# A transformer layer on one core: the context's first combination is rounded earlier, and one norm moves behind the last of seven products

## The chip, the core and the metric

The kernel runs on one core of a Trainium2 chip. The metric is the device time in microseconds (us) of one execution; the number reported is the median of several runs.

The engines go by short names: PE (TensorE, matmuls; PEld is its weight load), DVE (VectorE), ACT (ScalarE), POOL (GpSimd) and SP, whose queue issues the DMAs. Each works through its own queue in order and waits for the others through semaphores.

## The reference, cut to what matters

```python
def swiglu(h, w1, w3, w2):
    return (jax.nn.silu(h @ w1) * (h @ w3)) @ w2

def reference(...):
    ...
    x = x + 0.5 * m_l[2][:, None, :] * swiglu(modulate(rms_norm(x, norm1_w[i]), m_l[0], m_l[1]), ffn1_w1[i], ffn1_w3[i], ffn1_w2[i])
    ctx = ctx + 0.5 * m_c[2][:, None, :] * swiglu(modulate(rms_norm(ctx, norm1_w[i]), m_c[0], m_c[1]), ffn1_w1[i], ffn1_w3[i], ffn1_w2[i])
    y_l, y_c = token_mixing(modulate(rms_norm(x, norm2_w[i]), m_l[3], m_l[4]),
                            modulate(rms_norm(ctx, norm2_w[i]), m_c[3], m_c[4]), w_in[i], ...)
    x = x + m_l[5][:, None, :] * y_l
    x = x + 0.5 * m_l[8][:, None, :] * swiglu(modulate(rms_norm(x, norm3_w[i]), ...), ffn2_w1[i], ffn2_w3[i], ffn2_w2[i])
    ...
return rms_norm(x, final_norm_w)
```

One layer: a feed-forward block on 1024 latent tokens and on 256 context tokens (width 1024, hidden width 2816), a token mixing step whose latent scans start from the context's scan states, and a second feed-forward block on the latent tokens. Everything is float32. This case is about the second half of the first feed-forward block (the product with `w2`), and the norm (`norm2_w`) between it and the token mixing.

## The kernel before, in words

**Numbers in two parts.** A float32 tile is rounded to a high part on ACT (`whi`, `hh`; line 435) and the rest is taken on DVE (`wlo`, `hl`; line 436). `mm3` then makes three matmuls of a product: high with high (L440), low with high (L441) and high with low (L442). Together, the two instructions are called a split here.

**Seven products.** The tokens come in halves of 512 (groups 0 and 1 latent, group 2 the context). A big product of latent tokens is cut into two by two blocks and made with seven block products instead of eight, from sums and differences of blocks. `hidden` goes over pairs of hidden blocks f = 2, 4, ..., 20 (NF = 22) and makes, per pair, one chain of seven products with `w1` and one with `w3`, then the silu product and the sums that the next stage needs, which it stores to DRAM (`gd`). The adaLN columns (`ada`, line 511) are computed on DVE beside it. Scratch tiles of this stage are the 19 buffers with the tag `s`; a pair takes 14.

**The context's combinations.** The context's hidden values lie in DRAM (`cgd`) too. `ctx_comb(b)` loads four blocks (four DMAs), makes four differences on DVE and stores them (four DMAs), for b = 0, 1, 2; it runs after the pairs f of the tuple `COMB`. `ctx_load(i, b)` loads one combination for product i, and `ctx_split(i, b)` splits it.

**The product with w2.** Its seven products come in the order 1, 6, 5, 7, 3 (in `back_ctx`), then 2, then 4, each a loop over 11 pairs p (NP) of hidden blocks. A pair needs a split of its token block (`hh`, `hl`, four slots in turn) and one of its weights (`whi`, `wlo`), and is used by 12 matmuls into four banks (`psa` or `psb`). In the first five products three more matmuls per pair, into a fifth bank, take the context along: weights `whi`, `wlo` against the context's split tile (`s`, later `ch`, `cl`). Latent results are added to `x` (line 883).

**What sets the order.** A hand-written table `plan` names work that is emitted after pair number i of these 77 pairs; 5*NP (`p2`) is the first pair of product 2, 6*NP (`p4`) that of product 4. Within what is emitted, a scheduler sets each engine's order by priorities; SP's order in `back_ctx` is the written one. `NLOW` puts parts 1 and 2 of the norm of group 1 at a lower priority. From the step after product 4 on (`ctx_k`, the context's keys, and what follows) the operations are recorded first and ordered by a planner; in the profile they all have line 147.

**A norm** (`norm_part`) has these parts. 0: squares, summed in `nacc` (ACT and DVE). 1: four matmuls with a one-column result (L573, eight passes in the trace) into a bank taken by `psN`, then the root in two steps, `nr` on DVE (L1628) and POOL (L1629). 2: four diagonal tiles `ndiag` on DVE (L583), four matmuls of 128 columns on them (L592), a copy `nrb` on ACT. 3 and on, one for each of 8 feature blocks: `nt` on DVE (L606), `hh` on ACT (L607), `hl` on DVE (L618). Group 2 goes through it in product 2. Group 1 has part 0 and parts 1 and 2 there as well, and its eight blocks among the first pairs of product 4. Group 0 follows in the recorded part.

## Time and profile before

| what | value |
|---|---|
| median of 3 runs | 2083.25 us (2082.26, 2083.25, 2085.28) |
| the profiled execution | 2083.51 us, its span 2081.7 us |
| mean granted TensorE clock | 0.994 |
| PE busy | 2057.9 us, 99% |
| DVE busy | 1519.5 us, 73% |
| ACT busy | 984.4 us, 47% |
| POOL busy | 69.0 us, 3% |
| DMA | 376.39 MB, mean 181 GB/s |

A timeline row has the start in us from the span's start, the length in us, the engine, the line, the operation, output <- inputs, shapes and a count; in brackets stands how long the engine sat idle before it and what ended that. Matmuls are pipelined: a row is 0.39 us long while the next starts 0.23 us later. A row of a stretch gives from:to and its length, then the busy us (and instructions) of PE, PEld, DVE, ACT and POOL, the granted clock, the busy share of the DMA engines and GB/s.

### The profile page before, as it was taken

What the parts mean: (1) busy time and instruction counts of PE and PEld (TensorE: products, weight loads), DVE (VectorE), ACT (ScalarE), POOL (GpSimd) and SP (SyncE); (2) the same over time, 40 slices, a digit from 0 to 9 for tenths busy, and PEclk for the clock granted to TensorE, in tenths of its full rate; (3) what the DMA queues carried; (4) which work ended last, traced back from release to release, by engine and by line L of the source; (5) the groups of instructions that cost most, each with busy time, mean ns of one, the idle gap of its engine ahead of it and who ended that gap; (6) DMA issues with size and microseconds to landing.
All of it is one profiled execution on the core that took longest, in us unless ns stands there. A gap on an engine that the chain in (4) does not pass through costs nothing.

```text
span 2081.7 us, 33747 instructions
## 1 busy us (share of the span) xinstructions
PE 2057.9 (99%) x12137; PEld 1747.0 (84%) x12137; DVE 1519.5 (73%) x2775; ACT 984.4 (47%) x1819; POOL 69.0 (3%) x107
## 2 busy tenths in 40 slices
PE   9999999999999998999999999999999999999998
PEld 8998888888878887898788988888888888888888
DVE  5888788898867777765576478767776666766576
ACT  5765434433445445566475246444434344345553
POOL 0000000000000000001021001000000000010000
PEclk9999999999999999999999999999999999999999
DMA  9765565567779765664233233242344444477764
GB/s 362 231 198 165 182 197 197 196 232 260 248 275 320 254 226 166 196 202 137 68 113 93 83 89 107 87 162 81 111 157 147 146 163 157 151 240 236 218 228 152
DMA packets 210089, 376.39 MB, mean 181 GB/s; under 512 B 23937, under 2 KB 44161, under 8 KB 209793
## 3 DMA queue, kind: packets, MB, share of 16 engines
q1 hardware_dynamic: 209632, 374.10, 55.1%
q8 instruction: 95, 1.56, 0.3%
q14 instruction: 74, 0.60, 0.1%
q10 hardware_dynamic: 288, 0.13, 0.0%
HBM read 292.74 MB, written 73.01 MB: 176 GB/s over the span
## 4 chain that ended last, share of the span: by engine, by line
PE 92%; DVE 3%; DMA 3%; issue 1%; ACT 1%; SPq 0%; POOL 0%; DVEq 0%; POOLq 0%; ACTq 0%
PE psa L147 24%; PE psb L147 11%; PE psa L440 10%; PE psa L442 10%; PE psa L441 10%; PE psb L442 9%; PE psb L440 9%; PE psb L441 9%; DMA raw<-in_w 1%; DMA hh<-in_w 1%; DMA raw<-gd 1%; DVE hl L436 1%; DVE x L883 0%; DVE wlo L436 0%; DVE nt L147 0%
## 5 line engine op out<-in xcount | busy, mean ns | idle before, releaser
L435 ACT ACTIVATE whi<-raw 128x512 fp32r<-128x512 f32 x385 | 242.9, 631 | 507.1 <-issue 177.7
L436 DVE TENSOR_TENSOR wlo<-raw,whi 128x512 fp32r<-128x512 f32 x385 | 265.0, 689 | 152.2 <-ACT whi L435 145.6
L440 PE MATMUL psa<-hh,whi 128*128 128x512 f32 x676 | 265.1, 392 | 1.3 <-ACT nrb L2100 0.7
L441 PE MATMUL psa<-hl,whi 128*128 128x512 f32 x676 | 264.3, 391 | 0.0
L442 PE MATMUL psa<-hh,wlo 128*128 128x512 f32 x676 | 264.3, 391 | 0.0
L147 PE MATMUL psa<-hh,whi 128*128 128x512 f32 (+1 forms) x664 | 234.4, 354 | 0.9 <-ACT whi L147 0.5
L147 PE MATMUL psa<-hh,wlo 128*128 128x512 f32 (+1 forms) x664 | 233.3, 352 | 0.1
L147 PE MATMUL psa<-hl,whi 128*128 128x512 f32 (+1 forms) x664 | 233.1, 352 | 0.0
L440 PE MATMUL psb<-hh,whi 128*128 128x512 f32 x584 | 227.6, 390 | 0.0
L442 PE MATMUL psb<-hh,wlo 128*128 128x512 f32 x584 | 227.2, 389 | 0.0
L441 PE MATMUL psb<-hl,whi 128*128 128x512 f32 x584 | 227.2, 389 | 0.0
L147 DVE TENSOR_TENSOR wlo<-raw,whi 128x512 fp32r<-128x512 f32 (+1 forms) x217 | 139.4, 663 | 103.9 <-ACT whi L147 92.7
L147 ACT ACTIVATE whi<-raw 128x512 fp32r<-128x512 f32 (+1 forms) x217 | 130.1, 610 | 148.4 <-PE psa L147 111.8
L440 PEld LDWEIGHTS psa<-hh,whi 128*128 128x128 f32 x676 | 127.7, 189 | 28.4 <-ACT s L734 1.0
L442 PEld LDWEIGHTS psa<-hh,wlo 128*128 128x128 f32 x676 | 127.7, 189 | 26.8
L441 PEld LDWEIGHTS psa<-hl,whi 128*128 128x128 f32 x676 | 127.9, 189 | 26.6
L147 PEld LDWEIGHTS psa<-hh,whi 128*128 128x128 f32 x664 | 126.1, 190 | 17.7 <-ACT whi L147 1.0
L147 PEld LDWEIGHTS psa<-hh,wlo 128*128 128x128 f32 x664 | 126.0, 190 | 15.2 <-DVE wlo L147 0.3
L147 PEld LDWEIGHTS psa<-hl,whi 128*128 128x128 f32 x664 | 125.9, 190 | 14.8 <-issue 0.2
L442 PEld LDWEIGHTS psb<-hh,wlo 128*128 128x128 f32 x584 | 109.6, 188 | 22.7
L440 PEld LDWEIGHTS psb<-hh,whi 128*128 128x128 f32 x584 | 109.6, 188 | 22.6
L441 PEld LDWEIGHTS psb<-hl,whi 128*128 128x128 f32 x584 | 109.6, 188 | 22.6
(490 smaller groups left out, 4217.0 us busy)
## 6 DMA issues: line engine op xcount, KB each, us to landing
raw<-in_w SPq DMA_DIRECT2D x316, 256.0 KB, 3.4
gd<-s SPq DMA_DIRECT2D x154, 256.0 KB, 2.9
raw<-gd SPq DMA_DIRECT2D x102, 256.0 KB, 3.1
ada<-in_adaT SPq DMA_DIRECT2D x48, 512.0 KB, 4.0
s<-in_w SPq DMA_DIRECT2D x66, 256.0 KB, 4.6
hh<-in_w SPq DMA_DIRECT2D x55, 256.0 KB, 4.7
sd<-s SPq DMA_DIRECT2D x44, 256.0 KB, 2.9
raw<-sd SPq DMA_DIRECT2D x44, 256.0 KB, 3.6
```

What stands on the lines that cost most here:

```text
L147: self.rec.add(self.eng, lambda: f(*map(get, a), **{x: get(v) for x, v in k.items()}), outs, ins, name, a, k)
L435: nc.scalar.activation(hi, src, AF.Copy)
L436: (eng or nc.vector).tensor_tensor(out=lo, in0=src, in1=hi.bitcast(F32), op=ALU.subtract)
L440: mm(ps, wa[0], xa[0], start=start, stop=False, skip_group_check=more)
L441: mm(ps, wa[0], xa[1], start=False, stop=False, skip_group_check=more)
L442: return mm(ps, wa[1], xa[0], start=False, stop=stop, skip_group_check=more)
```

## The change

The three `ctx_comb` steps go one pair earlier (after f = 10, 12, 14). The load of the context's first combination for product 1 moves from behind `hidden` to the end of pair f = 16, its split to the end of pair f = 18. The bank choice `psN = psB` and parts 1 and 2 of the norm of group 1 move from product 2 into product 4 (pairs 1 and 4), and its eight blocks from pairs 0 to 7 to pairs 6 to 9.

```diff
-    def hidden(self, f0, mods=lambda: None, hold=False, comb=()):
+    def hidden(self, f0, mods=lambda: None, hold=False, comb={}):
...
             if f in comb:
-                self.ctx_comb(comb.index(f))
+                comb[f]()
...
-        self.hidden(F0, lambda: mods(MPER), True, COMB)
-        mods(2 * len(todo))
         self.craw, self.cw, self.xw, self.nbank = {}, {}, {}, -1
-        self.ctx_load(1, 0)
-        self.ctx_split(1, 0, f1)
+        comb = {f: lambda b=b: self.ctx_comb(b) for b, f in enumerate(COMB)}
+        comb[NF - 6] = lambda: self.ctx_load(1, 0)
+        comb[NF - 4] = lambda: self.ctx_split(1, 0, f1)
+        self.hidden(F0, lambda: mods(MPER), True, comb)
+        mods(2 * len(todo))
...
-        plan[p2 + 8].append(lambda: norm2(1, 1))
-        plan[p2 + 9].append(lambda: norm2(1, 2))
-        plan[p2 + 10].append(lambda: setattr(self, "psN", self.psB))
+        plan[p4 + 1] += [lambda: setattr(self, "psN", self.psB), lambda: norm2(1, 1)]
+        plan[p4 + 4].append(lambda: norm2(1, 2))
         for k in range(KD):
             plan[p2 + 7 + k // 2].append(lambda k=k: norm2(2, 3 + k))
-            plan[p4 + k].append(lambda k=k: norm1(k))
+            plan[p4 + 6 + k // 2].append(lambda k=k: norm1(k))
...
-COMB = (12, 14, 16)
+COMB = (10, 12, 14)
```

What this does to the engines' order is seen at three places. First PE in product 1, in the third pair before and behind the first pair now; `psb_6069` is the context's bank, `s_6019`/`s_6020` (now `s_5689`/`s_5690`) the high and low part of its split tile. Before:

```order
L440 MATMUL psa_6067<-hh_1242_6141,whi_6149 128x512
L441 MATMUL psa_6067<-hl_1243_6142,whi_6149 128x512
L442 MATMUL psa_6067<-hh_1242_6141,wlo_6150 128x512
L440 MATMUL psb_6069<-whi_6086,s_6019 128x512
L441 MATMUL psb_6069<-wlo_6087,s_6019 128x512
L440 MATMUL psa_6068<-hh_1242_6141,whi_6149 128x512
L442 MATMUL psb_6069<-whi_6086,s_6020 128x512
L440 MATMUL psb_6069<-whi_6116,s_6019 128x512
```

Now, at the end of the first pair (`whi_6086`):

```order
L440 MATMUL psa_6068<-hh_1223_6070,whi_6086 128x512
L441 MATMUL psa_6068<-hl_1224_6071,whi_6086 128x512
L442 MATMUL psa_6068<-hh_1223_6070,wlo_6087 128x512
L440 MATMUL psb_6069<-whi_6086,s_5689 128x512
L441 MATMUL psb_6069<-wlo_6087,s_5689 128x512
L442 MATMUL psb_6069<-whi_6086,s_5690 128x512
L440 MATMUL psa_6065<-hh_1234_6108,whi_6116 128x512
```

The context's matmuls of the first pairs stood together in the third pair and stand now behind their own pairs. Second PE at the norm of group 1. Before, between product 2 (`psb_8126`) and product 4 (`psa_8566`):

```order
L442 MATMUL psb_8126<-hh_1872_8489,wlo_8498 128x512
L573 MATMUL psa_8426<-ones_84,nacc_1735_7991 128x1 x4
L592 MATMUL psa_8466<-ndiag_8467,ones_84 128x128
L440 MATMUL psa_8566<-hh_1888_8570,whi_8578 128x512
L441 MATMUL psa_8566<-hl_1889_8571,whi_8578 128x512
```

Now, between product 4 (`psa_8546`) and the context's keys (`psb_8916`):

```order
L442 MATMUL psa_8546<-hh_1976_8869,wlo_8878 128x512
L573 MATMUL psb_8595<-ones_84,nacc_1735_7991 128x1 x4
L592 MATMUL psb_8675<-ndiag_8676,ones_84 128x128
L147 MATMUL psb_8916<-hh_1776_8184,whi_8909 128x256
L147 MATMUL psb_8916<-hl_1777_8185,whi_8909 128x256
```

The four column matmuls and the first diagonal one stand side by side in both; the place is later by the 132 matmuls of product 4. Third DVE behind the adds of product 4 (`x_1202`, `x_1203`). Before:

```order
L147 SCALAR_TENSOR_TENSOR x_1203_6042<-psa_8569,mod_88,x_1203_6042 128x512
L147 TENSOR_TENSOR nacc_1966_8834<-nacc_1966_8834,nsq_8929 128x512
L147 TENSOR_TENSOR wlo_8956<-raw_8895,whi_8913 128x512
L147 TENSOR_TENSOR nacc_1966_8834<-nacc_1966_8834,nsq_8946 128x512
L147 TENSOR_TENSOR wlo_8968<-raw_8897,whi_8921 128x512
L147 TENSOR_TENSOR nacc_1966_8834<-nacc_1966_8834,nsq_8960 128x512
```

Now:

```order
L1628 TENSOR_SCALAR nr_8600<-psb_8595 128x4
L147 SCALAR_TENSOR_TENSOR x_1203_6042<-psa_8546,mod_88,x_1203_6042 128x512
L147 TENSOR_TENSOR nacc_1960_8822<-nacc_1960_8822,nsq_8929 128x512
L147 TENSOR_TENSOR wlo_8956<-raw_8895,whi_8913 128x512
L583 TENSOR_SCALAR ndiag_8676<-ident_82,nr_8600 128x128
L147 TENSOR_TENSOR nacc_1960_8822<-nacc_1960_8822,nsq_8946 128x512
L583 TENSOR_SCALAR ndiag_8679<-ident_82,nr_8600 128x128
L583 TENSOR_SCALAR ndiag_8682<-ident_82,nr_8600 128x128
L147 TENSOR_TENSOR wlo_8968<-raw_8897,whi_8921 128x512
```

The root and the diagonals of group 1 stand now among the splits of the context's weights; eight `nt` and eight `hl` follow among the next ones, the last of them behind `wlo_9083`, the ninth low half of a context weight.

## The prediction

> **What bounds the kernel now.** I read the page first, then the busy time by stretches, then TensorE's (PE's) waits, then the order of time around each hole. The page gives the span and PE's share of it.

> ```profile
> span 2081.7 us, 33747 instructions
> PE 2057.9 (99%) x12137; PEld 1747.0 (84%) x12137; DVE 1519.5 (73%) x2775; ACT 984.4 (47%) x1819; POOL 69.0 (3%) x107
> ```

> PE is the bound: only 23.8 us of the span show no matmul. A change that removes no matmul can win only holes, and stretches at a lower clock. Next come two stretches that hold holes (columns: stretch, length, busy us of PE, PEld, DVE, ACT, POOL, granted clock, DMA share, GB/s) and the two longest waits of PE.

> ```profile
> 400.00:600.00 200.00, 196.95 (x852) 161.15 (x851) 174.17 (x309) 77.22 (x135) 1.64 (x1) 0.98 0.74 248
> 800.00:860.00 60.00, 53.21 (x236) 44.04 (x235) 44.88 (x83) 30.75 (x57) 2.58 (x2) 0.94 0.46 149
> ```

> ```profile
> PE psa L592 <- DVE ndiag L583: 6.1, 1, 6.1
> PE psb L147 <- issue: 2.2, 1, 2.2
> ```

> Both stretches lie where the change works, and in both the clock falls too. The timeline of PE at the start of the first of the seven products (start, length, instruction, in brackets the idle time and what ended it):

> ```profile
> 577.84 0.39 PE L440 MATMUL psa<-hh,whi 128*128 128x512 f32 x1
> ...
> 585.09 0.39 PE L442 MATMUL psa<-hh,wlo 128*128 128x512 f32 x1
> 586.84 0.50 PE L440 MATMUL psb<-whi,s 128*128 128x512 f32 x1 [1.36 <-ACT s L435]
> 587.17 0.40 PE L441 MATMUL psb<-wlo,s 128*128 128x512 f32 x1
> 587.40 0.40 PE L440 MATMUL psa<-hh,whi 128*128 128x512 f32 x1
> 589.50 0.79 PE L442 MATMUL psb<-whi,s 128*128 128x512 f32 x1 [1.69 <-DVE s L436]
> ...
> 595.53 0.40 PE L442 MATMUL psa<-hh,wlo 128*128 128x512 f32 x1
> 595.76 0.39 PE L440 MATMUL psa<-hh,whi 128*128 128x512 f32 x1
> ```

> From 577.84 to 585.09 stand 32 steps, 0.2267 us each. PE then waits for the context's s tiles, first the high part, then the low. From 589.50 to 595.53 there are 14 steps in 6.03 us instead of 3.17: half clock, 2.86 us. The matmul of 595.76 is the 51st after that of 577.84, so without the hole it would stand at 577.84 + 51 x 0.2267 = 589.40. **Hole A costs 6.36 us.** The second hole, between the products 2 and 4:

> ```profile
> 818.93 0.95 PE L573 MATMUL psa<-ones,nacc 128*128 128x1 f32 x8
> 825.99 0.80 PE L592 MATMUL psa<-ndiag,ones 128*128 128x128 f32 x2 [6.12 <-DVE ndiag L583]
> 826.44 0.77 PE L440 MATMUL psa<-hh,whi 128*128 128x512 f32 x1
> ...
> 831.12 0.40 PE L442 MATMUL psa<-hh,wlo 128*128 128x512 f32 x1
> ...
> 839.85 0.39 PE L440 MATMUL psa<-hh,whi 128*128 128x512 f32 x1
> ```

> 42 matmuls of product 4 stand between 818.93 and 839.85. Back to back the next would start at 818.93 + 42 x 0.2267 = 828.45. **Hole B costs 11.40 us**, norm passes included; 11 steps from 826.44 to 831.12 took 4.68 instead of 2.49 us, so 2.19 are half clock. Why it is so long the vector engine's and POOL's timelines show:

> ```profile
> 822.02 2.06 DVE L883 SCALAR_TENSOR_TENSOR x<-psb,mod,x 128x512 f32<-128x512 f32 x3
> 824.00 0.15 DVE L1628 TENSOR_SCALAR nr<-psa 128x4 f32<-128x4 f32 x1
> ...
> 825.65 0.87 DVE L583 TENSOR_SCALAR ndiag<-ident,nr 128x128 f32<-128x128 f32 x4 [0.90 <-POOL nr L1629]
> ```

> ```profile
> 824.24 1.38 POOL L1629 TENSOR_TENSOR nr<-nr,mhalf 128x4 f32<-128x4 f32 x1 [20.17 <-DVE nr L1628]
> ```

> PE waits first for DVE's queue (nr starts 5.07 us after L573), then for the chain nr, POOL, ndiag (1.65 us) and 0.34 us to the matmul.

> **The change part by part.** Edit one moves the load of the context's first combination, its split (one ACT and one DVE instruction) and the three ctx_comb steps ahead, into hidden pairs. In the new order the three psb matmuls stand right behind each pair, and the s tiles are written in the pair before last. What could be late next are the pairs' own operands. The slowest in the trace of before is the sixth pair's (pair 5, from 0) low half; below it stands the split that goes away.

> ```profile
> 587.46 0.69 DVE L436 TENSOR_TENSOR hl<-hh,hh 128x512 fp32r<-128x512 f32 x1
> ...
> 588.75 0.69 DVE L436 TENSOR_TENSOR s<-s,s 128x512 fp32r<-128x512 f32 x1
> ```

> It ends at 588.15; PE with 15 matmuls a pair asks for pair 5 at 577.84 + 5 x 3.40 = 594.84. Later pairs wait for slots that PE frees, so they move ahead with it. On SP one DMA leaves the queue ahead of later pair loads; the same DMA, and the combs' 12 loads and 12 stores, go past weight and ada loads in hidden. I cost them at nothing: the combs run inside the stretch 400 to 600 today, and its 3.05 us without PE are hole A alone. If that cover were gone, PE would wait for a weight split. Holding two of 19 s tiles one pair longer costs nothing while a pair takes 14. Edit one: -6.36, between 0 (the fourth rival) and the whole hole; I take the whole, by pair 5's margin of 6.7 us.

> Edit two removes hole B (-11.40) and puts the norm behind product 4. There PE again has the four L573 and the first L592 side by side, so a wait remains. Rows around that place today:

> ```profile
> 860.28 0.28 PE L147 MATMUL psb<-hh,whi 128*128 128x256 f32 x1
> ...
> 870.50 0.94 PE L147 MATMUL psb<-ones,nacc 128*128 128x1 f32 x8
> 871.31 0.36 PE L147 MATMUL psb<-hh,whi 128*128 128x256 f32 x1
> ```

> ```profile
> 855.02 1.41 DVE L606 SCALAR_TENSOR_TENSOR nt<-x,mod,nrb 128x512 f32<-128x512 f32 x2
> 856.56 1.42 DVE L618 SCALAR_TENSOR_TENSOR hl<-nt,mod,hh 128x512 fp32r<-128x512 f32 x2
> 858.44 2.79 DVE L147 SCALAR_TENSOR_TENSOR x<-psa,mod,x 128x512 f32<-128x512 f32 x4 [0.46 <-PE psa L442]
> 861.14 0.68 DVE L147 TENSOR_TENSOR nacc<-nacc,nsq 128x512 f32<-128x512 f32 x1
> 861.74 0.68 DVE L147 TENSOR_TENSOR wlo<-raw,whi 128x512 fp32r<-128x512 f32 x1
> ...
> 871.49 0.16 DVE L147 TENSOR_SCALAR nr<-psb 128x4 f32<-128x4 f32 x1 [0.59 <-PE psb L147]
> ```

> nr follows its L573 by 0.99 (870.50 to 871.49), so it starts at 860.28 + 0.99 = 861.27; the root ends 1.65 later, at 862.92. In order on DVE, x, nacc and wlo (0.70 + 0.60 + 0.60) let ndiag start at 863.2; PE follows 0.34 later, at 863.54. With this pass (0.18) and three more between the context's matmuls (0.15 each, an estimate from those 0.8 us per 8 small ones) the place costs 3.26 + 0.18 + 0.45 = **+3.9**. What hangs behind: 4 ndiag, 8 nt, 8 hl on DVE and nrb and 8 hh on ACT, until now in product 4, where nothing waited for them. They fall where DVE has this:

> ```profile
> 860.00:870.00 10.00, 10.00 (x82) 9.82 (x82) 7.25 (x12) 5.14 (x11) 0.00 (x0) 1.00 0.81 258
> 870.00:880.00 10.00, 10.00 (x87) 10.00 (x86) 6.19 (x16) 5.68 (x15) 1.33 (x1) 1.00 0.65 185
> 880.00:890.00 10.00, 10.00 (x82) 10.00 (x81) 10.00 (x17) 8.81 (x19) 0.00 (x0) 1.00 0.86 263
> ```

> From 860 to 880 that is 13.4 us of work in 20, and 16 x 0.70 + 0.87 = 12.1 come on top. Counted along the new order, from nr to the ninth weight split's low half (wlo_9083) stand 1 x, 4 nacc, 4 ndiag, 8 wlo, 8 nt, 6 hl, 2 nr: 0.67 + 2.4 + 0.8 + 4.8 + 5.4 + 4.0 + 0.2 = 18.3, so it is ready at 879.5. PE asks for it after 8 half weights of 12 matmuls at 0.122 (82 in 10 us) and one L573 group (0.81): 860.28 + 3.9 + 11.7 + 0.8 = 876.7, so it waits 2.8; two hl and the next wlo (1.9) take 0.5 longer than the 12 matmuls meanwhile (1.5): **+3.3**, bounds 0 (DVE runs ahead of need) and 12.1 (all exposed); I take the count, since it follows the order row by row. On ACT the nrb copy waits for the last L592 with the split whi_9003 behind it; PE wants that one only after six half weights (8.8 us), so this is free.

> Then the clock. PE does next to nothing from 860.4 to 863.5. Such holes today:

> ```profile
> 1018.89 0.33 PE L147 MATMUL psb<-zq,zk 128*32 128x32 f32 x7 [2.22 <-issue]
> ```

> ```profile
> 1019.00:1020.00 1.00, 1.00 (x53) 0.87 (x53) 0.00 (x0) 0.00 (x0) 0.00 (x0) 0.50 0.00 0
> ```

> A 2.22 us wait was followed by clock 0.50; so were 1.36 plus 1.69 in hole A. I take the drop here too, at the mean of 2.86 and 2.19: **+2.5**; bounds 0 and 2.9. [...]

> Sum against the profiled execution (2083.51, its span 2081.7 and 1.8 around it): -6.36 - 11.40 + 3.9 + 3.3 + 2.5 = -8.06, so 2075.45; the runs' median is 2083.25, 0.26 below, which gives 2075.2. The runs shown go from 2082.26 to 2085.28; 0.2% (4.2 us) is about what a measurement here can tell from no change.

> **The rivals.**
> - *The new hole keeps the clock.* All as forecast but the 2.5: 2072.7. For it: the new wait on ndiag (2.45 us from 861.09, where L573 lets go, to 863.54) is hardly longer than the shortest that shows a drop (2.22). 25%. [...]
> - *Neither clock nor backlog*: DVE and ACT keep ahead of the context's weights, since product 4 no longer loads them; only 3.9 remains: 2069.4. Against it: the count of 18.3 us. 8%.
> - *The stall just moves*: DVE comes to the boundary as late as at 819, the hole is as dear as hole B, and edit one alone pays: 2083.25 - 6.36 = 2076.9. 14%.
> - *Edit one does not do what it says*: another operand is late at 586 and hole A stays: 2081.6. Against it: the 6.7 us of margin of pair 5. 6%.
> - *DVE becomes the bound, slower*: the 12.1 us moved onto DVE lie wholly on PE's path in the context stage; with the 3.9 and a clock at half that its waits keep low (2.9) the norm costs 18.9 there, more than both holes (17.76): 2084.4. It decides from 17.8 on. For it: 880 to 900 is full on DVE already; against it: the idle third of 860 to 880. 5%.

> **How the numbers follow.** The forecast has 42%; its own range is 2073.5 to 2077. The range for 8 in 10 takes in the first three rivals: 2069 to 2079. Faster by over 0.2% means under 2079.1: forecast, the first three rivals: 0.89, less a little for holes that shifted DMAs may open in hidden: 0.87. Within 0.2%: the fourth rival and most of the slower one: 0.10. Slower: 0.03.

> **What the profile after would show.** Right: no wait on ACT s or DVE s at the start of product 1 and full clock there; product 4 directly behind product 2 with no L592 between; behind product 4 a wait of 2 to 3 us on ndiag, then half clock, then short waits of PE on wlo in the context stage. Wrong would be: a hole in the pairs of hidden between 400 and 570, pair operands late in product 1, a wait on ndiag near 6 us, or DVE full from 860 to 910 with PE waiting again and again.

## The result, and the profile after

| what | before | after |
|---|---|---|
| median of 8 runs each, in the same set | 2084.22 us (2081.11 to 2085.65) | 2074.78 us (2069.96 to 2080.07) |
| the profiled execution | 2083.51 us, span 2081.7 | 2074.48 us, span 2072.7 |

The ratio is 0.9958, with a 95% interval of 0.9946 to 0.9970: 6 to 11 us faster. A second set of five runs (the kernel `after_again` below) gave 2076.68 us and 0.9967 (0.9955 to 0.9980). The forecast was 2075.2 us, in a range of 2069 to 2079.

From the page of the changed kernel, and the two stretches that held the holes (columns as before):

```profile
span 2072.7 us, 33751 instructions
PE 2054.0 (99%) x12137; PEld 1745.8 (84%) x12137; DVE 1519.2 (73%) x2775; ACT 984.0 (47%) x1819; POOL 68.1 (3%) x107
```

```profile
400.00:600.00 200.00, 200.00 (x881) 164.31 (x880) 179.00 (x316) 81.04 (x143) 1.64 (x1) 1.00 0.74 246
800.00:860.00 60.00, 57.69 (x296) 49.95 (x296) 42.49 (x78) 30.47 (x57) 1.01 (x1) 0.97 0.56 180
```

The first stretch is now full for PE and at full clock (196.95 busy and 0.98 before). The second still has a hole, and it is another one. PE's longest waits (what waited, what for: total, times, longest):

```profile
PE psb L147 <- issue: 2.5, 1, 2.5
PE psb L592 <- DVE ndiag L583: 2.3, 1, 2.3
PE psb L147 <- DVE wlo L147: 2.1, 2, 1.7
```

PE's timeline in product 1: the context's matmuls stand behind their own pairs, 3.40 us apart, and wait for nothing. (Product 4 follows product 2 at 814.80 without a gap.)

```profile
582.76 0.39 PE L440 MATMUL psb<-whi,s 128*128 128x512 f32 x1
582.99 0.39 PE L441 MATMUL psb<-wlo,s 128*128 128x512 f32 x1
583.22 0.39 PE L442 MATMUL psb<-whi,s 128*128 128x512 f32 x1
...
586.16 0.39 PE L440 MATMUL psb<-whi,s 128*128 128x512 f32 x1
```

PE behind product 4, where the norm of group 1 is now:

```profile
844.49 0.39 PE L442 MATMUL psa<-hh,wlo 128*128 128x512 f32 x1
844.72 0.95 PE L573 MATMUL psb<-ones,nacc 128*128 128x1 f32 x8
847.98 0.49 PE L592 MATMUL psb<-ndiag,ones 128*128 128x128 f32 x2 [2.31 <-DVE ndiag L583]
848.22 0.37 PE L147 MATMUL psb<-hh,whi 128*128 128x256 f32 x1
...
862.27 0.39 PE L147 MATMUL psb<-hh,wlo 128*128 128x256 f32 x1 [0.33 <-DVE wlo L147]
...
863.57 0.28 PE L147 MATMUL psb<-hl,whi 128*128 128x256 f32 x1
865.59 0.58 PE L147 MATMUL psb<-hh,wlo 128*128 128x256 f32 x1 [1.74 <-DVE wlo L147]
```

The clock in two stretches, one behind each of the two longer waits:

```profile
848.46:851.87 3.41, 3.41 (x19) 3.41 (x18) 3.41 (x9) 0.63 (x1) 0.00 (x0) 0.50 0.49 151
865.52:868.93 3.41, 3.34 (x15) 3.34 (x16) 3.41 (x8) 1.04 (x3) 0.88 (x1) 0.50 0.35 105
```

And DVE there, from the root to the ninth low half of a context weight (`wlo` at 864.86):

```profile
845.70 0.16 DVE L1628 TENSOR_SCALAR nr<-psb 128x4 f32<-128x4 f32 x1 [0.71 <-PE psb L573]
...
847.64 0.28 DVE L583 TENSOR_SCALAR ndiag<-ident,nr 128x128 f32<-128x128 f32 x1
...
853.69 1.42 DVE L606 SCALAR_TENSOR_TENSOR nt<-x,mod,nrb 128x512 f32<-128x512 f32 x2 [1.57 <-ACT nrb L2101]
...
864.86 0.68 DVE L147 TENSOR_TENSOR wlo<-raw,whi 128x512 fp32r<-128x512 f32 x1
```

The last matmul starts 9.1 us earlier. Where that comes from is seen by comparing the start of the same matmul, counted from the first of 12137, in both traces:

| matmuls | part of the program | after less before, us |
|---|---|---|
| 1 to 301 | start of the program | +2.29 |
| 301 to 3301 | hidden | -0.08 |
| 3301 to 3451 | start of product 1 (hole A) | -6.37 |
| 3451 to 4201 | products 1 to 3 | +0.03 |
| 4201 to 4801 | products 2 and 4, context's keys (hole B, and the new place) | -1.77 |
| 5401 to 5851 | around the third half clock stretch of before | -2.36 |
| the rest | | -0.80 |

What the change touches gives -8.14 (forecast: -8.06). The first and the sixth row are not put down to the change. In the first lie a half clock stretch at 19.02 us (3.41 long) and a 0.92 us wait for a DMA at 18.85, which the trace of before lacks; in the sixth lies the stretch at 1018.66, which the trace after lacks, but which the same kernel has in `after_again` (1014.26).

### The profile page after: what moved, and what is told of

Its sections match the earlier page's. It is cut to its first block, busy times and chain, and to the rows that moved or that the text cites. A ratio compares the mean times of both kernels' runs of the same rounds, so it can differ in the third digit from the quotient of the medians.

```text
span 2072.7 us, 33751 instructions
## 1 busy us (share of the span) xinstructions
PE 2054.0 (99%) x12137; PEld 1745.8 (84%) x12137; DVE 1519.2 (73%) x2775; ACT 984.0 (47%) x1819; POOL 68.1 (3%) x107
## 4 chain that ended last, share of the span: by engine, by line
PE 96%; DVE 2%; DMA 1%; ACT 0%; issue 0%; SPq 0%; POOLq 0%; DVEq 0%; ACTq 0%
PE psa L147 24%; PE psa L440 11%; PE psa L442 11%; PE psa L441 11%; PE psb L147 10%; PE psb L440 9%; PE psb L442 9%; PE psb L441 9%; DMA ada<-in_adaN 1%; DVE nt L147 0%; DVE hl L147 0%; DVE nt L606 0%; PE psb L1957 0%; DMA rs<-rq 0%; DVE S L147 0%
## 5 line engine op out<-in xcount | busy, mean ns | idle before, releaser
L435 ACT ACTIVATE whi<-raw 128x512 fp32r<-128x512 f32 x385 | 243.1, 632 | 516.4 <-issue 181.6
L436 DVE TENSOR_TENSOR wlo<-raw,whi 128x512 fp32r<-128x512 f32 x385 | 264.8, 688 | 159.5 <-ACT whi L435 153.3
L440 PE MATMUL psa<-hh,whi 128*128 128x512 f32 x676 | 263.3, 390 | 0.6 <-ACT s L734 0.6
L442 PE MATMUL psa<-hh,wlo 128*128 128x512 f32 x676 | 263.1, 389 | 0.0
L441 PE MATMUL psa<-hl,whi 128*128 128x512 f32 x676 | 263.0, 389 | 0.0
L147 PE MATMUL psa<-hh,whi 128*128 128x512 f32 (+1 forms) x664 | 234.3, 354 | 0.7 <-ACT whi L147 0.4
L147 PE MATMUL psa<-hh,wlo 128*128 128x512 f32 (+1 forms) x664 | 233.2, 352 | 0.1
L147 PE MATMUL psa<-hl,whi 128*128 128x512 f32 (+1 forms) x664 | 232.9, 351 | 0.0
L440 PE MATMUL psb<-hh,whi 128*128 128x512 f32 x584 | 227.6, 390 | 0.0
L442 PE MATMUL psb<-hh,wlo 128*128 128x512 f32 x584 | 227.2, 389 | 0.0
L441 PE MATMUL psb<-hl,whi 128*128 128x512 f32 x584 | 227.2, 389 | 0.0
L147 DVE TENSOR_TENSOR wlo<-raw,whi 128x512 fp32r<-128x512 f32 (+1 forms) x217 | 139.6, 662 | 102.0 <-ACT whi L147 92.5
L147 ACT ACTIVATE whi<-raw 128x512 fp32r<-128x512 f32 (+1 forms) x217 | 130.3, 609 | 151.6 <-PE psa L147 112.1
L440 PEld LDWEIGHTS psa<-hh,whi 128*128 128x128 f32 x676 | 126.9, 188 | 27.3 <-ACT s L734 1.0
L442 PEld LDWEIGHTS psa<-hh,wlo 128*128 128x128 f32 x676 | 126.9, 188 | 26.3
L441 PEld LDWEIGHTS psa<-hl,whi 128*128 128x128 f32 x676 | 126.9, 188 | 26.3
L147 PEld LDWEIGHTS psa<-hh,whi 128*128 128x128 f32 x664 | 126.2, 190 | 17.5 <-issue 1.0
L147 PEld LDWEIGHTS psa<-hh,wlo 128*128 128x128 f32 x664 | 126.0, 190 | 15.1 <-DVE wlo L147 0.3
L147 PEld LDWEIGHTS psa<-hl,whi 128*128 128x128 f32 x664 | 125.8, 190 | 14.8 <-DVE wlo L147 0.4
L442 PEld LDWEIGHTS psb<-hh,wlo 128*128 128x128 f32 x584 | 109.6, 188 | 22.7
L440 PEld LDWEIGHTS psb<-hh,whi 128*128 128x128 f32 x584 | 109.7, 188 | 22.6
L441 PEld LDWEIGHTS psb<-hl,whi 128*128 128x128 f32 x584 | 109.6, 188 | 22.6
```

Source lines behind the costliest of these rows:

```text
L147: self.rec.add(self.eng, lambda: f(*map(get, a), **{x: get(v) for x, v in k.items()}), outs, ins, name, a, k)
L435: nc.scalar.activation(hi, src, AF.Copy)
L436: (eng or nc.vector).tensor_tensor(out=lo, in0=src, in1=hi.bitcast(F32), op=ALU.subtract)
L440: mm(ps, wa[0], xa[0], start=start, stop=False, skip_group_check=more)
L441: mm(ps, wa[0], xa[1], start=False, stop=False, skip_group_check=more)
L442: return mm(ps, wa[1], xa[0], start=False, stop=stop, skip_group_check=more)
```

## The experiments

Times are medians. Each ratio compares the runs with those of the kernel before in the same set (median 2084.22 us for `after`, 2082.07 for the four kernels from `edit_one` on, 2082.38 for the next four, 2083.25 for the last two); it is not the quotient of the two medians, and the savings in us given with an interval are worked out from it. "A" is the time from the 3151st to the 3601st matmul (hole A lies in it), "norm" that from the 4201st to the 4901st (products 2 and 4 and the context's keys), both from the trace, with the time at half clock in brackets.

| kernel | us | ratio (95%) | A | norm |
|---|---|---|---|---|
| before | 2084.22 | | 108.37 (6.83) | 126.43 (6.83) |
| after | 2074.78 | 0.9958 (0.9946 to 0.9970) | 102.13 (0) | 124.66 (6.82) |
| edit_one | 2077.43 | 0.9973 (0.9962 to 0.9984) | 102.12 (0) | 126.56 (6.83) |
| edit_two | 2081.70 | 0.9995 (0.9983 to 1.0007) | 108.90 (6.83) | 123.00 (3.41) |
| norm_in_p4 | 2065.54 | 0.9918 (0.9899 to 0.9937) | 102.17 (0) | 116.81 (0) |
| root_early | 2074.78 | 0.9956 (0.9940 to 0.9972) | 102.13 (0) | 124.78 (3.41) |
| late_blocks | 2074.50 | 0.9961 (0.9949 to 0.9974) | 102.17 (0) | 123.85 (3.41) |
| root_early_late_blocks | 2071.13 | 0.9944 (0.9932 to 0.9957) | 102.13 (0) | 120.36 (3.41) |
| norm_in_p2 | 2067.73 | 0.9927 (0.9914 to 0.9941) | 102.17 (0) | 117.16 (0) |
| after_again | 2076.68 | 0.9967 (0.9955 to 0.9980) | 102.13 (0) | 125.78 (10.24) |
| load_early_only | 2080.59 | 0.9985 (0.9977 to 0.9994) | 106.27 (3.41) | 126.14 (6.83) |
| norm_in_p4_again | 2066.20 | 0.9912 (0.9898 to 0.9925) | 102.17 (0) | 116.82 (0) |

### Each edit alone

`edit_one` is the change without the hunk on `plan` (the norm stays in product 2); `edit_two` is that hunk alone.

> Only the first part of the change: the context's first combination is loaded and split inside hidden, the norm of group 1 stays between the products 2 and 4. Base: 2084.2 before (median of 8 runs). Theory (the two holes add up): hole A is gone, hole B stays, so 6.4 less: 2077.9, a ratio of 0.9969. PE shows no wait on s at the start of product 1 and the 6.1 us wait on ndiag at 0.81 to 0.83 ms as before. Rival (edit one does not do what it says, the norm brings all): 2084. Rival (the holes are not independent, one moves into the other): 2081 or above, with a wait on ndiag longer than 6.1 us.

> Only the second part: the norm of group 1 moves into product 4 and ends behind it; hole A stays. Theory: 11.4 us of hole B go, 9.7 come back behind product 4 (3.9 place, 3.3 backlog, 2.5 clock as forecast; the trace after shows 3.9, 2.4 and 3.4), so 1.7 less than 2084.2: 2082.5. Rival (stall as dear as before): 2084.2. Rival (edit two brings most of the 9.4): 2077 or less. Rival (no half clock behind product 4): 2079 to 2080.

Edit one alone is 5.6 us faster (3.3 to 7.9), 6.25 in stretch A of its trace; hole B is as it was:

```profile
PE psa L592 <- DVE ndiag L583: 6.2, 1, 6.2
```

Edit two alone is 1.0 us faster (0.4 by the medians), with an interval from 3.5 faster to 1.5 slower, so the runs alone do not tell it from nothing. Its trace does not show the stall as dear as before: the wait on ndiag is 2.31 us, and the norm stretch is 3.4 shorter, 1.7 of that (an estimate, half of 3.41) because one half clock stretch of 3.41 is missing. The rival in which edit two brings most of the gain is out.

### What made hole A: the load or the queue

```diff
-        comb[NF - 4] = lambda: self.ctx_split(1, 0, f1)
...
         mods(2 * len(todo))
+        self.ctx_split(1, 0, f1)
```

(against `edit_one`)

> A part of edit one: the combination for product 1 is loaded in hidden (and the combs run a pair earlier), but its split stays behind hidden, where the kernel before has it; the norm of group 1 is as before. In the trace before ACT's split waits 1.33 us for the load's landing, and DVE's split stands behind an adaLN column (1.28 us) and small steps until 588.75. Theory (hole A needs both, since DVE's queue holds the low part whenever the load lands): the wait on ACT goes, the wait on DVE s grows from 1.7 to 2 to 3 us, half clock stays: 0 to 1.5 us less than before, 2081 to 2082.5. Rival (the load alone made hole A): 5.5 to 6.4 less, as in the kernel edit_one (2077.4).

It came out between the two, at 3.1 us faster (1.2 to 4.8), and not as the theory had it (0 to 1.5, with a longer wait on DVE). In the trace, stretch A is 2.1 shorter, 1.7 of it (again half of 3.41) because 3.41 us at half clock stand where 6.83 stood; without the clock, 0.4. PE's two waits there:

```profile
585.41 0.50 PE L440 MATMUL psb<-whi,s 128*128 128x512 f32 x1 [2.07 <-ACT s L435]
588.83 0.79 PE L442 MATMUL psb<-whi,s 128*128 128x512 f32 x1 [0.18 <-DVE s L436]
```

The long wait is now the one on ACT, whose split follows without a gap on the splits of the pairs:

```profile
584.22 0.61 ACT L435 ACTIVATE hh<-hl 128x512 fp32r<-128x512 f32 x1
584.74 0.61 ACT L435 ACTIVATE s<-s 128x512 fp32r<-128x512 f32 x1
```

DVE's split comes 0.66 earlier than before, and PE, at half clock from 586.08, gets there only then:

```profile
588.09 0.68 DVE L436 TENSOR_TENSOR s<-s,s 128x512 fp32r<-128x512 f32 x1
```

So the late load was the smaller part of hole A in the trace (2.1 of 6.3, most of it clock); how large a part, the runs do not settle (3.1, from 1.2 to 4.8). The rest is the place of the split in the queues of ACT and DVE, and its move into hidden is what took that away.

### The stall and the backlog, apart

Two kernels differ from the changed one in the priorities of group 1's norm, in one line of `norm_step`. `norm_in_p4` (the first added line) was to have neither stall nor backlog, `root_early` (the second) only the backlog:

```diff
-            with self.low(NLOW if tg == 1 and i in (1, 2) else None):
+            with self.low(None):
+            with self.low(NLOW if tg == 1 and i == 2 else None):
```

> The changed kernel with one difference: parts 1 and 2 of the norm of group 1 have no lower priority, so the four column matmuls stand in the first pair of product 4 and the diagonals 36 matmuls (8 us) behind them, and its blocks run on DVE inside product 4. Theory: wait, backlog and half clock behind product 4 (9.6 in the trace after) all vanish, only the passes themselves stay (about 1.4), so 8.2 less than 2074.8: 2066.6. Rival (product 4 has no room on DVE for the norm): waits of PE on weight splits in product 4, 2070 to 2075. Rival (the column matmuls wait for a bank of product 2): a hole of 1 to 2 us at the start of product 4, with the clock 2069 to 2070.

> The changed kernel with one difference: the column matmuls and the root of group 1's norm run in product 4, the diagonals (L592), the copy and the eight blocks stay behind product 4. So the stall is taken away and the backlog on DVE is left. Additive sum of the forecast: the place loses 3.1 to 3.5 and the first half clock stretch 1.7 to 2.5, the waits on wlo (2.4 in the trace after) stay: 2069 to 2070. Theory after the trace: DVE sets PE there, and PE, 3.1 us earlier, waits longer for the ninth low half; DVE gains only the idle 1.6 us and the diagonals' 0.8: 2070 to 2072.5. Rival (DVE is the bound there, nothing is won): 2074 to 2075.

`norm_in_p4` came out as expected, at 2065.5 us. In its trace PE is full from 800 to 860, the diagonals stand 9 us behind the column matmuls, and neither has an idle time in its row:

```profile
821.92 0.95 PE L573 MATMUL psb<-ones,nacc 128*128 128x1 f32 x8
830.99 1.06 PE L592 MATMUL psb<-ndiag,ones 128*128 128x128 f32 x8
```

```profile
800.00:860.00 60.00, 60.00 (x322) 51.96 (x321) 50.59 (x93) 35.85 (x66) 2.87 (x3) 1.00 0.58 191
```

`root_early` is the surprise. The stall (3.26 us from the column matmuls to the first diagonal one, 2.31 of them a wait) and the half clock behind it are gone, and nothing is won (ratio 0.9956; the norm stretch 124.78 against 124.66). PE reaches the context's weights sooner and waits for them, by 5.9 us in place of 2.1:

```profile
855.39 0.39 PE L147 MATMUL psb<-hh,wlo 128*128 128x256 f32 x1 [2.78 <-DVE wlo L147]
858.64 0.39 PE L147 MATMUL psb<-hh,wlo 128*128 128x256 f32 x1 [1.57 <-DVE wlo L147]
861.89 0.39 PE L147 MATMUL psb<-hh,wlo 128*128 128x256 f32 x1 [1.55 <-DVE wlo L147]
```

In these 20 us DVE has no gap, and PE 5.9 us without a matmul:

```profile
843.80:863.70 19.90, 14.00 (x107) 13.08 (x105) 19.90 (x31) 13.42 (x24) 0.00 (x0) 1.00 0.42 143
```

The rival "DVE is the bound there" is right, and both sums, the forecast's and mine after the trace, are wrong here: they took 2 to 6 us for the stall, and the run won nothing. The run does a little more than take the stall away, though. Its blocks start earlier on DVE (the first nt at 850.07, in the kernel after at 853.69), and all sixteen stand ahead of the ninth low half (864.25), where two hl stood behind it:

```profile
850.07 1.41 DVE L606 SCALAR_TENSOR_TENSOR nt<-x,mod,nrb 128x512 f32<-128x512 f32 x2
...
864.25 1.90 DVE L147 TENSOR_TENSOR wlo<-raw,whi 128x512 fp32r<-128x512 f32 x3
```

So the three waits are on the fifth, sixth and seventh low half, not on the ninth as expected. What the stall alone would be worth with DVE's order unchanged is not shown.

### Less backlog

`late_blocks` (the first added line) is the changed kernel, and `root_early_late_blocks` (the second) is `root_early`, with a lower priority for the eight blocks, so that fewer of them stand ahead of the ninth low half on DVE:

```diff
-            with self.low(NLOW if tg == 1 and i in (1, 2) else None):
+            with self.low(NLOW if tg == 1 and i in (1, 2) else 300 if tg == 1 and i > 2 else None):
+            with self.low({2: NLOW}.get(i, 300 if i > 2 else None) if tg == 1 else None):
```

> The changed kernel with one difference: the eight feature blocks of group 1's norm have a lower priority (300), so 4 nt and 3 hl stand behind the ninth low half of a context weight on DVE (4.7 us of DVE work less ahead of it); the diagonals 2 to 4 come 35 matmuls later. The stall behind product 4 stays, the backlog is cut. Theory (DVE paces PE behind product 4): the waits on wlo (2.4) and the second half clock stretch (1.7) go, 2070.7 from 2074.8. Rival (the same DVE work only waits later): a wait on wlo or on nt, hl between 870 and 900, 2073.5 to 2075. Rival (additive sum of the forecast): 3.3 less, 2071.5.

> Both differences together: the root runs in product 4 (no stall behind it) and the blocks have the lower priority, so ahead of the ninth low half stand 4 nt and 2 hl where the kernel root_early has 8 and 8 (10 x 0.67 = 6.7 us of DVE work less). Theory (behind product 4 PE is paced by DVE: the waits of 5.9 us in root_early are DVE's queue): they go nearly all, and with them the half clock stretch, 2074.8 less 5.9 and 1.7: 2067.2. Rival (the sum of DVE work up to 900 counts, not its order): 2071 to 2075, with waits later in the context stage. Rival (taking the stall away is worth nothing by itself, as in root_early): equal to the kernel late_blocks.

`late_blocks` missed the theory's 2070.7: it is at 2074.5 us, 2.2 under the changed kernel of the same set, with overlapping intervals. The waits on `wlo` behind product 4 did go (0.69 and 0.22 are left, at 876 and 880), but the order of DVE changed ahead of them too. The first diagonal now stands behind three adds and three weight splits, 3.69 us after nr (1.94 in the kernel after), and the stall grew from 2.31 to 4.06:

```profile
844.84 0.16 DVE L1628 TENSOR_SCALAR nr<-psb 128x4 f32<-128x4 f32 x1
...
848.53 0.47 DVE L583 TENSOR_SCALAR ndiag<-ident,nr 128x128 f32<-128x128 f32 x2
```

```profile
848.86 0.64 PE L592 MATMUL psb<-ndiag,ones 128*128 128x128 f32 x2 [4.06 <-DVE ndiag L583]
```

With both differences it is 2071.1 us, against 2074.5 for `late_blocks` and 2076.7 for the kernel after; the theory's 2067.2 is missed, and the rival with waits later (2071 to 2075) fits. The norm stretch is 4.4 shorter than that of `root_early`: 6.7 us of DVE work taken from ahead of PE's need bought 4.4. Most of the rest came back 9 us later, at a split of the next weights, with a half clock stretch of 3.41 us behind it:

```profile
870.51 0.40 PE L147 MATMUL psa<-wlo,hh 128*128 128x288 f32 x1 [1.96 <-DVE wlo L147]
```

With the blocks held back, taking the stall away was thus worth 3.4 us (2074.5 to 2071.1); without that, it was worth nothing.

### The norm left in product 2, and two repeats

`norm_in_p2` is `edit_one` with the same line set to `self.low(None)`.

> Edit one, and the norm of group 1 left where the kernel before has it, in product 2, but without the lower priority of its parts 1 and 2: the column matmuls stand in pair 8 of product 2 and 13 matmuls (2.9 us) ahead of the diagonals; its blocks are in the first pairs of product 4. Theory (hole B is the two side by side on PE, and a late DVE queue, not the product): the chain of nr, POOL, ndiag and two splits between them on DVE takes 3.3 to 4.5, so 0 to 1 us of wait, with half clock at most 1.7 more: 2065.5 to 2068.5. Rival (product 2 has no room on DVE, group 2's norm runs there too): waits on weight splits, 2070 or more. Rival (the move into product 4 itself is worth the most): 2074.

It is at 2067.7 us, inside the theory's range. The diagonals stand 3.85 us behind the column matmuls (810.33 and 814.18), with 13 matmuls between, and come 0.2 us later than back to back. Hole B was not in the product in which the norm was done; it was in the lower priority of its parts 1 and 2, which let the column matmuls and the diagonals meet at the end of a product.

> The changed kernel unchanged, for a second trace and more times: 2074.8. If the half clock behind product 4 belongs to the hole, both stretches (848.5 and 865.5 in the first trace) are there again, and no run has a mean clock over 0.997. If it is a matter of how the hole lies to a clock decision that runs on its own period (in the kernel edit_two the first of the two is missing), one of them or the one near 1015 comes and goes, and the run's time goes with its mean clock: 0.001 of 2072 us is 4.1 us of half clock, 2.1 us of time.

> The kernel norm_in_p4 unchanged, for a second trace and more times. If its gain is the stall, the backlog and the half clock behind product 4, the stretch from product 2 to the keys of the context shows full clock and no wait over 1 us again: 2064 to 2067. If it was luck with the clock, half clock shows there now: 2068 to 2071.

`norm_in_p4` held (2066.2, full clock in the norm stretch). Of the two kernels that beat the changed one clearly, it is the faster by its medians, but the intervals of the two overlap. In `after_again` PE's order is that of the first trace, and from 842 to 848 us its times are too, to a hundredth, but the clock drops at 847.01 for 6.83 us where it dropped at 848.46 for 3.41; in `edit_two`, with the same wait, it does not drop there:

```profile
855.11 0.49 PE L592 MATMUL psb<-ndiag,ones 128*128 128x128 f32 x2 [2.31 <-DVE ndiag L583]
```

```profile
847.01:853.84 6.83, 5.86 (x27) 5.87 (x28) 5.11 (x12) 1.26 (x2) 0.00 (x0) 0.50 0.33 115
```

```profile
851.80:855.20 3.40, 1.09 (x10) 0.97 (x9) 2.69 (x7) 2.34 (x5) 1.01 (x1) 1.00 0.77 286
855.20:858.70 3.50, 3.50 (x30) 3.50 (x31) 3.50 (x9) 0.63 (x1) 0.00 (x0) 1.00 0.44 136
```

(The wait in `edit_two`, where the place is at 851.86; then the clock in `after_again`, then in `edit_two`.) The expectation of `after_again` is not decided by that run alone. As its first half has it, both stretches are there again, and no run of this set has a mean clock over 0.996; as its second half has it, the one near 1015, missing in the first trace, has come. For the second half speak the changed length at the same wait, and `edit_two`.

## Why the prediction was right, and where its steps were not

- **Hole A: -6.36.** Measured -6.24 in stretch A, -5.6 (3.3 to 7.9) in the runs of `edit_one`. The step stands whole: the pairs' own operands are in time, and hidden moved by 0.08 us, so the combs and their DMAs are free there.
- **Hole B out, -11.40, and +9.7 back.** The net of -1.70 was measured as -1.77 in the first trace, -0.65 in the second (more half clock), -3.43 in the trace of `edit_two` (less half clock), and -1.0 (with an interval that holds 0) in its runs.
- **The place, +3.9.** From L573 to the first matmul of the keys 3.50 us (844.72 to 848.22), and three more passes; the wait was 2.31 where 2.45 was forecast.
- **The backlog, +3.3.** Waits of 0.33 and 1.74. The count of DVE's work from nr to the ninth low half was 18.3; the trace has 845.70 to 865.54, 19.84, of which 1.57 is idle behind nrb, so 18.27 of work. That idle time was not foreseen, and the half clock (3.41 us from 848.46) delays PE's demand, which the sum did not take in; the two errors partly cancel.
- **The clock, +2.5.** Mis-sized: two stretches of 3.41 us cost at most 3.4 in the first trace, 10.24 us at most 5.1 in the second (an estimate: half the time at half clock; less where PE waits in it). The second stretch, behind the wait on `wlo`, was not in the sum at all.
- **What failed is the addition.** The sum treats place, clock and backlog as three prices. `root_early` shows that the stall and the half clock behind it can be taken away and the same time is left: behind product 4 DVE sets the pace (busy 19.90 of 19.90 us), and what PE does not wait for at the diagonals it waits for at the weights. Taken away together, as in `norm_in_p4`, they are worth 124.66 - 116.81 = 7.9. That the 9.7 came out near as a whole fits one cause behind all three, 12.1 us of DVE work put where PE needs DVE, but is in part luck with the clock. It is the mechanism of the rival "DVE becomes the bound", given 5%, at far less than its price of 18.9.
- **The other rivals.** "The stall just moves" is out by the trace (2.31, not 6.1); its time, 2076.9, alone would not tell it from the 2076.68 of `after_again`. "Edit one does not do what it says" is out by `edit_one`, "neither clock nor backlog" by the waits on `wlo` and the two stretches. "The new hole keeps the clock" is what `edit_two` shows at the first wait; by these three executions it is a matter of the run more than of the kernel.
- **The nearness of 2074.78 to 2075.2** is partly luck: `after_again` gave 2076.68, and the gain over before was, by the medians, 9.4 us in one set and 5.7 in the other, both with intervals that hold the forecast's 8.0. The two edits alone add up to 6.6. In the traces the parts that the change does not touch happen to cancel but for 0.9.

## What to carry to other kernels

When work is moved out of a hole, count what its vector instructions delay at the new place, and treat that delay and the stall at the place as one queue: removing the visible stall alone can be worth nothing (2074.78 us in `root_early`, as in the kernel after). A chain PE - vector engine - PE is hidden when enough matmuls stand between its two ends (13 left 0.2 us here, 36 nothing), and a lower priority for both ends does the opposite, since it collects them side by side at the next boundary (a wait of 6.2 us in `edit_one`, 2.31 in the kernel after). The better version of this change lets that chain run inside a product at normal priority: 2065.5 us in product 4, 2067.7 in product 2, which the runs do not tell apart.

## What the runs showed of the hardware

That moves a run's time: at half clock for h us, up to h/2 is lost (an estimate: in before, 14 steps from 589.50 on took 6.03 us in place of 3.17) and the mean clock falls by h/2 over the span, so 0.001 of mean clock is up to 2.07 us. The fastest run of the kernel after (2069.96) has a mean clock of 0.999, the slowest (2080.07) 0.994: 10.4 by this estimate, 10.1 measured. It is not the whole spread: with the lost share of the clock taken off, the eight runs still go from 2064.6 to 2068.3.

Waits shorter than such a step were followed by half clock: 2.31 and 1.74 us (848.46 and 865.52 in after). What decides it these runs do not settle: in `root_early` a step in which PE had no matmul for 1.72 us (853.93 to 857.34, two steps ahead of the half clock that its rows show from about 864.2) was followed by full clock (1.00 up to 863.70), in `after_again` one with 1.35 us and the one-column matmuls beside (843.60 to 847.01) by half clock.
